# Second layer's decay matrices as one exponential with 0/1 masks in the batches, and later transposes of finished outputs

## The chip, the cores and the metric

One core of a Trainium2 chip. The time is the device time of one launch in microseconds (us), median of three runs. The engines are named as the profile names them: PE (TensorE matmuls), PEld (its weight loads), DVE (VectorE), ACT (ScalarE), POOL (GpSimd), SP (SyncE, which here issues loads).

## What is computed

One step of a two-layer encoder over 1024 prompt frames and 64 sample frames, width 1024, in fp32. The first layer (gated convolution and band attention) is not touched. The second is gated DeltaNet: 8 heads, 17 chunks of 64 frames (16 of the prompt, one of the sample). For a head and chunk, with `gc` the running sum of the log decays:

```
decay = exp(where(l >= m, gc[l] - gc[m], -inf))
a     = where(l > m, beta[l] * (k k^T) * decay, 0)
sol   = solve(I + a, [v * beta, k * beta * exp(gc)])
u     = sol_v - sol_k @ S
qk    = (q k^T) * decay
o     = (q * exp(gc)) @ S + qk @ u
S     = exp(gc[-1]) * S + (k * exp(gc[-1] - gc))^T @ u
y     = rmsnorm(o) * silu(z) @ w_out
```

The gates are negative, so `gc` falls within a chunk, and for l >= m the difference is the negative of its absolute value.

## The kernel before

Everything is transposed: channels on the 128 partitions, the 1088 frames in the free dimension, in three groups of 384, 384 and 320 frames. A projection (`project`, lines around L186) multiplies a 128x1024 weight tile with one group, each fp32 operand split into a high and a low part: per group 24 matmuls, in the profile `pjt<-hhi,whi`, `pjt<-hhi,wlo` and `pjt<-hlo,whi`. These fill TensorE. The weights are split by ScalarE (L164) and VectorE (L165).

The order of TensorE is written by a small planner, `Order`: each piece of work is a generator with a rank and a list of what must be done before it. A piece that yields a number is not looked at again until the plan's own clock (nanoseconds, advanced by an estimate per matmul) has moved on that much; of the pieces that are due, the lowest rank goes next. The projections (`main`, rank 5) fill what the rest leaves. So a number in a `yield` says how many nanoseconds of other TensorE work are planned between two steps. The order of the other engines comes from the framework's scheduler when the program is built; each engine then runs its list in order.

In the second layer (`odd`) the heads go in four pairs (p = 0 to 3), one head on each half of the partitions, and the chunks of a pair in three batches of 6, 6 and 5. The profile calls batch b of pair p number n = 3p + b. Per batch:

- `gates` once at the start makes `gc` and its exponentials (`G`).
- `decays` (L886 on, once for all pairs, rank 3): per pair and batch, VectorE spreads `gc` over an identity (`gx`, L895), TensorE sums it over the rows of a head, which broadcasts it (a matmul into `tr`), VectorE subtracts `gc` (`df`, L899). Then twice: GpSimd adds a mask of 0 and -1e30 (L902), ScalarE takes the exponential (L903), a transfer stores it in HBM (L904, `Dd`). The first result is strictly lower triangular (for `a`), the second is upper triangular with the diagonal (for `qk`, transposed). All of it lives in one buffer, `dbuf`, in parts.
- `prepare` (rank 2; waits for `dec{p}`, the pair's decays): SyncE loads both matrices (`Dst`, `DT`, L930 and L931); TensorE transposes k and q of the batch (`tr<-cst,kq`), ScalarE sums their squares (`junk`, L945) and copies k (`kt`), VectorE makes `kd` (L948), then the reciprocal root of the sums by a shift and three Newton steps of small operations (`rr`, `rt`, L747 to L753), then `sT`, `sA` and `kap`; GpSimd scales `kt` (L957). TensorE multiplies k with k and q (`tr<-kq`, two groups, 8 and 4 or 2 matmuls). VectorE makes `An` from the first half (L966, times `sA` and `Dst`) and `KQD` from the second (L967, times `DT`), and picks the diagonal 16x16 blocks of `An` into `Af` (L971, L973), which go through HBM (`Sd`) to another layout.
- `substitute` inverts those blocks on GpSimd (`px`, `AL`, L991 and L992), `join` builds the 64x64 inverse (`X`, `XT`, `M`), `solve` (`BD`, `vr`) applies it.
- `scan` (rank 1) carries the state S over the chunks (`ks`, `us`, `su`) and makes the outputs `o`, four chunks to a tile `o4` (three buffers); before a fourth tile it waits for the `finish` of the first.
- `finish` (rank 3): VectorE and GpSimd make the reciprocal root for the norm (`so`, L747 to L758), VectorE scales `o` (L1175); then `yield 9000`; then TensorE transposes it (`tr<-cst,o`), ScalarE scales it by the norm's weights (L1183) and it is stored (`od`).

All these share two PSUM buffers named `tr`: TensorE's next write to one waits until the engines that read its last content are done. Dst, DT and (after the change) E have a single buffer in SBUF, `An` two, `KQD` three.

Of the kernel before, what the change touches and what calls it, by code (L numbers as in the profile page):

```python
# [15 lines left out]
P = 128  # L16
# [23 lines left out]
C_M1, C_M2 = 448, 512  # L40
# [16 lines left out]
def constants():  # L57
    c = np.zeros((P, NCONST), np.float32)
    p = np.arange(P)
    h, i = p // 64, p % 64  # L60
    same = h[:, None] == h[None, :]
    c[:, C_ID:C_ID + P] = np.eye(P)
    c[:, C_U:C_U + P] = same & (i[:, None] <= i[None, :])
    c[:, C_BD:C_BD + P] = same
    c[:, C_H:C_H + 2] = h[:, None] == np.arange(2)[None, :]
    j = np.arange(64)
    c[:, C_ID64:C_ID64 + 64] = i[:, None] == j[None, :]
    c[:, C_M1:C_M1 + 64] = np.where(j[None, :] < i[:, None], 0.0, NEG)
    c[:, C_M2:C_M2 + 64] = np.where(j[None, :] >= i[:, None], 0.0, NEG)
    c[:, C_B16:C_B16 + 4] = (i // 16)[:, None] == np.arange(4)[None, :]  # L70
    c[:, C_H16:C_H16 + 2] = (i // 16 % 2)[:, None] == np.arange(2)[None, :]
    return c
# [35 lines left out]
class Net:  # L108
# [121 lines left out]
    def run(self):  # L230
# [4 lines left out]
        with tc.tile_pool(name="pj", bufs=2, space=PSUM) as self.pj:  # L235
# [15 lines left out]
            self.Dd = [dram.tile([P, NCH, 64], F32, name=f"Dd{i}") for i in range(8)]  # L251
# [481 lines left out]
    def odd(self):  # L733
# [147 lines left out]

        def decays():
            gc = G["gc"]
            buf = G["buf"]

            def part(i, m):  # L886
                return buf[:, 384 * i:384 * i + 64 * m].rearrange("p (c j) -> p c j", j=64)

            for p in range(4):
                yield 0  # L890
                for c0, m in BATCHES:
                    sh = [P, m, 64]
                    gcb = gc[:, p, c0:c0 + m].unsqueeze(2).broadcast_to(sh)
                    gx, df = part(0, m), part(1, m)
                    dve.tensor_tensor(gx, gcb, cst[:, C_ID64:C_ID64 + 64].unsqueeze(1).broadcast_to(sh), ALU.mult)  # L895
                    yield 900
                    ps = pst("tr")
                    self.mm(ps[:, :64 * m], cst[:, C_BD:C_BD + P], gx.rearrange("p c j -> p (c j)"))
                    dve.tensor_tensor(df, ps[:, :64 * m].rearrange("p (c j) -> p c j", j=64), gcb, ALU.subtract)  # L899
                    for q, (cm, op) in enumerate(((C_M1, ALU.subtract), (C_M2, ALU.add))):  # L900
                        dx = part(2 + q, m)
                        pool.tensor_tensor(dx, cst[:, cm:cm + 64].unsqueeze(1).broadcast_to(sh), df, op)  # L902
                        act.activation(dx, dx, AF.Exp)  # L903
                        nc.scalar.dma_start(Dd[2 * p + q][:, c0:c0 + m, :], dx)  # L904
# [11 lines left out]
        def prepare(p, b):  # L916
# [3 lines left out]
            yield 4000 if b == 0 else 0  # L920
# [8 lines left out]
            Dst, DT = bt("Dst", 64), bt("DT", 64)  # L929
            nc.sync.dma_start(Dst, Dd[2 * p][:, c0:c0 + nb, :])  # L930
            nc.sync.dma_start(DT, Dd[2 * p + 1][:, c0:c0 + nb, :])  # L931
# [26 lines left out]
            An, KQD = bt("An", 64, 2), bt("KQD", 64, 3)  # L958
            for i0 in range(0, nb, 4):
# [5 lines left out]
                for i in range(m):  # L965
                    dve.scalar_tensor_tensor(An[:, i0 + i, :], ps[:, i, 0:64], sA[:, i0 + i:i0 + i + 1], Dst[:, i0 + i, :], ALU.mult, ALU.mult)  # L966
                dve.tensor_tensor(KQD[:, i0:i0 + m, :], ps[:, :m, 64:128], DT[:, i0:i0 + m, :], ALU.mult)  # L967
# [4 lines left out]
            for j in range(1, 4):  # L972
                dve.scalar_tensor_tensor(Af, An[:, :, 16 * j:16 * j + 16], cst[:, C_B16 + j:C_B16 + j + 1], Af, ALU.mult, ALU.add)  # L973
            sa = Sd[0][b]
# [190 lines left out]
        def finish(p, b, i0, m, o4, so):  # L1165
# [10 lines left out]
            yield 9000  # L1176
# [10 lines left out]
        def add_pair(p):  # L1187
            for b in range(NB):
# [8 lines left out]
                order.add(f"prep{n}", 2, prepare(p, b), [f"dec{p}"] + after("prep", n - 1) + after("wy", n - 2) + after("scan", n - 3))  # L1197
# [136 lines left out]
```

## Time and profile before

| | us |
|---|---|
| median of 3 runs (range) | 1455.97 (1453.89 to 1456.44) |
| profiled execution | 1450.93 |
| its span, first to last instruction | 1449.1 |
| PE busy | 1372.1 |
| DVE busy | 877.6 |
| ACT busy | 678.0 |
| POOL busy | 312.9 |

Times in the profile count from the first instruction of the span. A busy share is an average over stages with different limits, so it is read by stretches. "Idle before" an instruction is put down to the one that released it last. The granted clock is TensorE's, 1.00 being full speed. The second layer's decays run from about 694 us (first `gx`) to 777 us (last store), its last scan ends well before the output projections.

### The profile page before, as it was taken

The numbers are of one execution on the slowest core, as the hardware profiler recorded it, in microseconds if no ns is written. First come the engines' busy times: TensorE is split into PE (matmuls) and PEld (weight loads), VectorE is DVE, ScalarE is ACT, GpSimd is POOL, SyncE is SP. The second block draws the span as 40 slices with busy tenths as digits, with TensorE's granted clock in tenths as the row PEclk, the third lists the DMA queues.
The fourth block names the chain that finished last, engine by engine and source line by source line (L and its number), as shares of the span: only waits on it lengthen the run. The fifth ranks groups of instructions, "written<-read, shape, count | busy, mean of one in ns | idle before, by whom it ended". The sixth has DMA issues, their size and how long they took to land. (4 is left out here: it accounts for less than half of the span.)

```text
span 1449.1 us, 28440 instructions
## 1 busy us (share of the span) xinstructions
PE 1372.1 (95%) x10600; PEld 1233.9 (85%) x10600; DVE 877.6 (61%) x2497; ACT 678.0 (47%) x1776; POOL 312.9 (22%) x810
## 2 busy tenths in 40 slices
PE   8999999999999999899878999999899989998996
PEld 6989998998999899888768778788887877888985
DVE  7675257137435754777887768676765756433654
ACT  7643345144334456675546444544453534323642
POOL 3000000000100014420345325140523152210322
PEclk9999999999999999999989999999999999999998
DMA  7402111210210274541523112122211232337454
GB/s 260 143 16 89 57 52 52 80 53 26 90 61 30 66 244 135 190 140 37 119 73 79 40 29 77 33 52 44 68 30 31 62 95 67 95 123 234 141 197 162
DMA packets 114378, 133.12 MB, mean 92 GB/s; under 512 B 35568, under 2 KB 81336, under 8 KB 114240
## 3 DMA queue, kind: packets, MB, share of 16 engines
q1 hardware_dynamic: 83280, 105.01, 24.8%
q10 hardware_dynamic: 30960, 26.31, 5.6%
q8 instruction: 83, 1.36, 0.4%
q14 instruction: 55, 0.45, 0.1%
HBM read 99.91 MB, written 34.51 MB: 93 GB/s over the span
## 5 line engine op out<-in xcount | busy, mean ns | idle before, releaser
L119 PE MATMUL pjt<-hhi,wlo 128*128 128x384 f32 (+1 forms) x1768 | 617.7, 349 | 1.5 <-DVE wlo L165 1.5
L119 PE MATMUL pjt<-hhi,whi 128*128 128x384 f32 (+1 forms) x1768 | 583.7, 330 | 5.8 <-ACT whi L164 2.4
L119 PE MATMUL pjt<-hlo,whi 128*128 128x384 f32 (+1 forms) x1768 | 576.1, 330 | 0.7 <-DVE hlo L391 0.6
L119 PEld LDWEIGHTS pjt<-hhi,wlo 128*128 128x128 f32 x1768 | 337.6, 191 | 25.6 <-issue 11.7
L119 PEld LDWEIGHTS pjt<-hhi,whi 128*128 128x128 f32 x1768 | 337.6, 191 | 12.4 <-ACT whi L164 3.7
L119 PEld LDWEIGHTS pjt<-hlo,whi 128*128 128x128 f32 x1768 | 335.6, 190 | 1.8 <-DVE hlo L391 1.8
L165 DVE TENSOR_TENSOR wlo<-wf,whi 128x512 fp32r<-128x512 f32 x222 | 154.3, 721 | 153.0 <-ACT whi L164 149.5
L164 ACT CAST whi<-wf 128x512 fp32r<-128x512 f32 x222 | 129.6, 618 | 165.0 <-PE pjt L119 123.4
L612 ACT ACTIVATE pr<-pr,mx 128x640 f32<-128x640 f32 (+5 forms) x72 | 50.9, 707 | 89.4 <-DVE mx L611 88.9
L784 DVE SCALAR_TENSOR_TENSOR kq<-pjt,par,kq 128x384 f32<-128x384 f32 (+2 forms) x144 | 71.6, 497 | 2.9
L348 POOL TENSOR_TENSOR sqa<-sqa,sq 128x384 f32<-128x384 f32 (+1 forms) x36 | 39.7, 1103 | 151.7 <-ACT sq L346 151.6
L573 POOL MEMSET bias<- 64x64 f32 x8 | 1.3, 163 | 321.0 <-DMA bias<-Gd 228.2
L609 DVE CUSTOM_DVE_ANT_0 pr<-sc,bias 128x640 f32<-128x640 f32 (+5 forms) x72 | 48.0, 666 | 26.7 <-PE sc L119 25.9
L991 POOL TENSOR_TENSOR px<-AL 48x14 f32<-48x14 f32 (+6 forms) x168 | 46.9, 279 | 61.5 <-DMA AL<-Sd 52.5
L1154 DVE SCALAR_TENSOR_TENSOR S<-S,egl,su 128x128 f32<-128x128 f32 x128 | 40.6, 343 | 29.3 <-PE su L119 28.9
L755 POOL TENSOR_TENSOR so<-so 128x4 f32<-128x4 f32 (+2 forms) x72 | 16.7, 232 | 175.4 <-DVE so L748 117.2
L945 ACT ACTIVATE junk<-tr 128x128 f32<-128x128 f32 x136 | 37.7, 277 | 33.9 <-PE tr L124 29.6
L992 POOL TENSOR_TENSOR AL<-AL,px 48x14 f32<-48x14 f32 (+6 forms) x168 | 46.8, 278 | 9.4
L119 PE MATMUL pjt<-mhi,whi 128*128 128x384 f32 x128 | 44.4, 347 | 3.7 <-ACT mhi L164 3.7
L124 PE MATMUL pt<-cst,pr 128*128 128x128 f32 (+1 forms) x280 | 43.4, 270 | 4.5 <-DVE pr L614 2.9
L1113 ACT ACTIVATE junk<-o 128x128 f32<-128x128 f32 x68 | 21.0, 309 | 51.4 <-DVE o L1109 42.2
L119 PE MATMUL pjt<-mlo,whi 128*128 128x384 f32 x128 | 44.5, 348 | 0.3 <-DVE mlo L165 0.2
(250 smaller groups left out, 2210.8 us busy)
## 6 DMA issues: line engine op xcount, KB each, us to landing
wf<-in_w_in SPq DMA_DIRECT2D x128, 256.0 KB, 3.5
wf<-in_w_out SPq DMA_DIRECT2D x96, 256.0 KB, 3.5
mf<-mixd SPq DMA_DIRECT2D x32, 192.0 KB, 3.4
x<-in_x SPq DMA_DIRECT2D x8, 384.0 KB, 6.2
xg<-in_x SPq DMA_DIRECT2D x2, 1536.0 KB
xd<-xg SPq DMA_DIRECT2D x2, 1536.0 KB
Dd<-dbuf ACTq DMA_DIRECT2D x16, 192.0 KB, 2.1
od<-o ACTq DMA_DIRECT2D x12, 256.0 KB, 2.5
```

The costliest lines, as they stand in the source:

```text
L119: return self.pe.matmul(out, lhsT=lhsT, rhs=rhs, start=start, stop=stop, **k)
L124: return self.pe.transpose(out, in_, self.ident[0:k, 0:k])
L164: self.act.copy(out=hi, in_=x)
L165: (eng or self.dve).tensor_tensor(lo, x, hi.bitcast(F32), ALU.subtract)
L348: pool.tensor_tensor(acc, acc, sq, ALU.add)
L609: dve.tensor_tensor_reduce(out=cut(pr[0:nq, :nk]), in0=sc[0:nq, :nk // nw, :nw], in1=cut(b["bias"][a][0:nq, j0:j0 + nk]), scale=1.0, scala ...
L612: act.activation(pr[0:nq, :nk], pr[0:nq, :nk], AF.Exp, bias=mx[0:nq, 1:2], scale=1.0, accum_out=mx[0:nq, 2:3])
L784: dve.scalar_tensor_tensor(oi, ch(ps[:, i0 + j + 1:i0 + j + 1 + m]), cw[j], oi, ALU.mult, ALU.add)
L945: act.activation(junk, ps[:, i, :], AF.Square, accum_out=ss[:, a, i0 + i:i0 + i + 1])
L991: pool.tensor_tensor(t, AL[:, j + 1:16, j:j + 1].broadcast_to([lanes, m, w]), x.broadcast_to([lanes, m, w]), ALU.mult)
L992: pool.tensor_tensor(o, o, t, ALU.add)
L1154: dve.scalar_tensor_tensor(Sn[:, q, :], S[:, q, :], egl[:, q, p, c:c + 1], su[q], ALU.mult, ALU.add)
```

## The change

Since the decay is symmetric up to the mask, `decay` now makes one matrix E = exp(-|difference|) per pair and batch: the same spread, matmul and subtraction, but the difference stays in PSUM (written in place), ScalarE takes its absolute value and then the exponential; no mask. For the pairs 1 to 3 it is made in `decays` and goes through HBM as before, one store (L905) and one load (L932) instead of two. For the pair 0 `prepare` makes it itself, with `An` as scratch for `gx`, and so waits for `gates` only.

The masks are now 0 and 1 and are multiplied: GpSimd makes `KQD` = E times the upper mask (L963) ahead of VectorE's product with q k^T; `An` takes E unmasked, and the strict lower mask is applied to `Af`, whose 16x16 blocks are the only place where it matters (the other blocks that are used lie wholly below the diagonal). And `finish` waits 15000 instead of 9000 before its transposes, but for the last batch.

```diff
-    c[:, C_M1:C_M1 + 64] = np.where(j[None, :] < i[:, None], 0.0, NEG)
-    c[:, C_M2:C_M2 + 64] = np.where(j[None, :] >= i[:, None], 0.0, NEG)
+    c[:, C_LOW:C_LOW + 16] = j[None, :16] < (i % 16)[:, None]
+    c[:, C_UP:C_UP + 64] = j[None, :] >= i[:, None]
...
+        def decay(e, gx, p, c0, m):
+            sh = [P, m, 64]
+            gcb = G["gc"][:, p, c0:c0 + m].unsqueeze(2).broadcast_to(sh)
+            dve.tensor_tensor(gx, gcb, cst[:, C_ID64:C_ID64 + 64].unsqueeze(1).broadcast_to(sh), ALU.mult)
+            yield 900
+            ps = pst("tr")[:, :64 * m]
+            self.mm(ps, cst[:, C_BD:C_BD + P], gx.rearrange("p c j -> p (c j)"))
+            ps = ps.rearrange("p (c j) -> p c j", j=64)
+            dve.tensor_tensor(ps, ps, gcb, ALU.subtract)
+            act.activation(e, ps, AF.Abs)
+            act.activation(e, e, AF.Exp, scale=-1.0)
...
-            for p in range(4):
-                yield 0
+            for p in range(1, 4):
                 for c0, m in BATCHES:
...
-                    dve.tensor_tensor(df, ps[:, :64 * m].rearrange("p (c j) -> p c j", j=64), gcb, ALU.subtract)
-                    for q, (cm, op) in enumerate(((C_M1, ALU.subtract), (C_M2, ALU.add))):
-                        dx = part(2 + q, m)
-                        pool.tensor_tensor(dx, cst[:, cm:cm + 64].unsqueeze(1).broadcast_to(sh), df, op)
-                        act.activation(dx, dx, AF.Exp)
-                        nc.scalar.dma_start(Dd[2 * p + q][:, c0:c0 + m, :], dx)
+                    e = piece(2 + i % 3, m)
+                    yield from decay(e, piece(i % 2, m), p, c0, m)
+                    nc.scalar.dma_start(Dd[p][:, c0:c0 + m, :], e)
+                    i += 1
                     yield 2500
...
-            yield 4000 if b == 0 else 0
...
-            Dst, DT = bt("Dst", 64), bt("DT", 64)
-            nc.sync.dma_start(Dst, Dd[2 * p][:, c0:c0 + nb, :])
-            nc.sync.dma_start(DT, Dd[2 * p + 1][:, c0:c0 + nb, :])
+            E, An, KQD = bt("E", 64), bt("An", 64, 2), bt("KQD", 64, 3)
+            if p:
+                nc.sync.dma_start(E, Dd[p][:, c0:c0 + nb, :])
+            else:
+                yield from decay(E, An, p, c0, nb)
+            if b == 0:
+                yield 4000
...
-            An, KQD = bt("An", 64, 2), bt("KQD", 64, 3)
+            pool.tensor_tensor(KQD, E, cst[:, C_UP:C_UP + 64].unsqueeze(1).broadcast_to([P, nb, 64]), ALU.mult)
...
-                dve.tensor_tensor(KQD[:, i0:i0 + m, :], ps[:, :m, 64:128], DT[:, i0:i0 + m, :], ALU.mult)
+                dve.tensor_tensor(KQD[:, i0:i0 + m, :], ps[:, :m, 64:128], KQD[:, i0:i0 + m, :], ALU.mult)
...
+            dve.tensor_tensor(Af, Af, cst[:, C_LOW:C_LOW + 16].unsqueeze(1).broadcast_to([P, nb, 16]), ALU.mult)
...
-            yield 9000
+            yield 9000 if p == 3 and b == NB - 1 else 15000
...
-                order.add(f"prep{n}", 2, prepare(p, b), [f"dec{p}"] + after("prep", n - 1) + after("wy", n - 2) + after("scan", n - 3))
+                order.add(f"prep{n}", 2, prepare(p, b), [f"dec{p}" if p else "gates"] + after("prep", n - 1) + after("wy", n - 2) + after("scan", n - 3))
```

More of the change, by code (lines that the diff above doesn't have):

```diff
@@ L39 @@
 C_ID64 = 384
-C_M1, C_M2 = 448, 512
+C_LOW, C_UP = 448, 512
 C_B16 = 576
@@ L250, in run @@
             self.Gd = [dram.tile([P, LROW], F32, name=f"Gd{h}") for h in range(8)]
-            self.Dd = [dram.tile([P, NCH, 64], F32, name=f"Dd{i}") for i in range(8)]
+            self.Dd = [dram.tile([P, NCH, 64], F32, name=f"Dd{i}") for i in range(4)]
             self.Sd = [[dram.tile([m, P, 16], F32, name=f"Sd{a}{b}") for b, (c0, m) in enumerate(BATCHES)] for a in range(2)]
@@ L880, in gates, with piece @@
             yield 1500
+        def decay(e, gx, p, c0, m):
[9 more added lines that the diff above has]
+            act.activation(e, e, AF.Exp, scale=-1.0)
         def decays():
-            gc = G["gc"]
-            buf = G["buf"]
-            def part(i, m):
+            buf, i = G["buf"], 0
+            def piece(i, m):
                 return buf[:, 384 * i:384 * i + 64 * m].rearrange("p (c j) -> p c j", j=64)
-            for p in range(4):
-                yield 0
+            for p in range(1, 4):
                 for c0, m in BATCHES:
[L892 to L899, printed above, removed]
-                    for q, (cm, op) in enumerate(((C_M1, ALU.subtract), (C_M2, ALU.add))):
-                        dx = part(2 + q, m)
-                        pool.tensor_tensor(dx, cst[:, cm:cm + 64].unsqueeze(1).broadcast_to(sh), df, op)
-                        act.activation(dx, dx, AF.Exp)
-                        nc.scalar.dma_start(Dd[2 * p + q][:, c0:c0 + m, :], dx)
+                    e = piece(2 + i % 3, m)
+                    yield from decay(e, piece(i % 2, m), p, c0, m)
+                    nc.scalar.dma_start(Dd[p][:, c0:c0 + m, :], e)
+                    i += 1
                     yield 2500
@@ L965, in prepare @@
                 for i in range(m):
-                    dve.scalar_tensor_tensor(An[:, i0 + i, :], ps[:, i, 0:64], sA[:, i0 + i:i0 + i + 1], Dst[:, i0 + i, :], ALU.mult, ALU.mult)
-                dve.tensor_tensor(KQD[:, i0:i0 + m, :], ps[:, :m, 64:128], DT[:, i0:i0 + m, :], ALU.mult)
+                    dve.scalar_tensor_tensor(An[:, i0 + i, :], ps[:, i, 0:64], sA[:, i0 + i:i0 + i + 1], E[:, i0 + i, :], ALU.mult, ALU.mult)
+                dve.tensor_tensor(KQD[:, i0:i0 + m, :], ps[:, :m, 64:128], KQD[:, i0:i0 + m, :], ALU.mult)
                 yield 510
```

## The prediction

> **What bounds the kernel now.** First the page's busy shares, then the chain that ended last, then a table by stretches of the second layer, then TensorE's waits in each stretch.
>
> ```profile
> PE 1372.1 (95%) x10600; PEld 1233.9 (85%) x10600; DVE 877.6 (61%) x2497; ACT 678.0 (47%) x1776; POOL 312.9 (22%) x810
> PE 9%; DMA 3%; DVE 2%; ACT 1%; issue 0%; DVEq 0%; SPq 0%; ACTq 0%
> ```
>
> TensorE is busy for 95% of the span and its order is fixed when the program is built. The chain is only the tail. So the end moves by what TensorE loses: stalls in its order, and time at a reduced clock. The change leaves TensorE's work alone (the same matmuls and transposes), so I look where it loses. In the windows below the columns are length, then busy time and count of each engine, then the granted clock. The first stretch, 689 to 777 us, is where the old decays run (their first and last masked operands fall in it); the second is the rest of the batches.
>
> ```profile
> 689.00:777.00 88.00, 71.35 (x398) 63.53 (x397) 71.56 (x180) 44.91 (x124) 37.78 (x61) 0.90 0.40 97
> 777.00:1240.00 463.00, 441.69 (x4558) 368.33 (x4559) 311.41 (x1146) 213.66 (x727) 152.90 (x586) 0.99 0.23 54
> 721.70:725.10 3.40, 3.40 (x12) 3.34 (x11) 3.19 (x10) 1.93 (x8) 1.26 (x1) 0.50 0.52 181
> 738.80:742.20 3.40, 2.95 (x10) 2.38 (x10) 2.22 (x9) 1.77 (x10) 0.00 (x0) 0.50 0.36 116
> 749.00:752.40 3.40, 3.40 (x13) 3.40 (x12) 2.69 (x9) 1.82 (x7) 0.94 (x1) 0.50 0.76 75
> 762.70:769.50 6.80, 4.75 (x14) 4.17 (x15) 5.86 (x20) 3.43 (x6) 5.89 (x13) 0.50 0.25 77
> 1172.72:1175.70 2.98, 2.98 (x11) 2.94 (x12) 0.82 (x5) 0.84 (x2) 0.21 (x1) 0.50 0.73 136
> ```
>
> The first stretch loses 88.00 - 71.35 = 16.65 us to stalls in 88 us; the second loses 21.3 us in 463. Four windows of the first stretch, 17.0 us together, ran at clock 0.50; TensorE was busy in 14.5 us of them (3.40 + 2.95 + 3.40 + 4.75), so they cost half of that, 7.25 us. The last row is one such window in the second stretch: 2.98 us at half speed, 1.5 us lost. Who is waited for, in the first stretch and then in the second:
>
> ```profile
> PE tr L119 <- DVE KQD L967: 4.5, 1, 4.5
> PE tr L124 <- DVE dbuf L899: 4.0, 2, 2.6
> PE tr L124 <- DVE KQD L967: 3.4, 1, 3.4
> PE tr L119 <- DVE dbuf L895: 2.6, 2, 1.6
> PE tr L119 <- ACT junk L945: 1.5, 2, 0.9
> ...
> PE tr L124 <- DVE o L1175: 4.4, 2, 3.1
> PE su L119 <- DVE us L1140: 3.3, 2, 2.6
> PE tr L119 <- POOL AL L992: 2.6, 1, 2.6
> ```
>
> Nearly all are waits for one of the two PSUM buffers named `tr`, held until VectorE has read it. VectorE is late in that stretch (busy 71.56 of 88). Why, the groups of VectorE and GpSimd show, for the first stretch and then (the rows after the dots) for the second:
>
> ```profile
> L899 DVE TENSOR_TENSOR dbuf<-tr,gc 128x384 f32<-128x384 f32 x8 | 4.4, 555 | 3.2 <-PE tr L119 2.4 <-POOL dbuf L902 0.8
> L752 DVE TENSOR_TENSOR rt<-rt,rr 128x12 f32<-128x12 f32 x6 | 4.3, 710 | 0.1
> L753 DVE SCALAR_TENSOR_TENSOR rr<-rt,rr 128x12 f32<-128x12 f32 x6 | 2.0, 327 | 0.2
> L902 POOL TENSOR_TENSOR dbuf<-cst,dbuf 128x384 f32<-128x384 f32 x16 | 18.2, 1153 | 62.5 <-DVE dbuf L899 54.4 <-DMA Dd<-dbuf 7.7 <-issue 0.3
> L902 POOL TENSOR_TENSOR dbuf<-cst,dbuf 128x320 f32<-128x320 f32 x8 | 8.0, 1016 | 13.9 <-DVE dbuf L899 8.8 <-ACT whi L164 3.4 <-DMA Dd<-dbuf 1.7
> L903 ACT ACTIVATE dbuf<-dbuf 128x384 f32<-128x384 f32 x16 | 8.4, 525 | 15.1 <-POOL dbuf L902 15.0
> ...
> L752 DVE TENSOR_TENSOR rt<-rt,rr 128x12 f32<-128x12 f32 x18 | 3.3, 183 | 0.2
> L753 DVE SCALAR_TENSOR_TENSOR rr<-rt,rr 128x12 f32<-128x12 f32 x18 | 3.2, 177 | 0.3
> ```
>
> A twelve-column product takes 183 ns where there are no decays and 710 ns beside them. One case in the timeline (start, length) shows how:
>
> ```profile
> 759.41 2.47 DVE L752 TENSOR_TENSOR rt<-rt,rr 128x12 f32<-128x12 f32 x1
> ...
> 759.65 0.99 POOL L902 TENSOR_TENSOR dbuf<-cst,dbuf 128x384 f32<-128x384 f32 x1
> 760.61 0.28 POOL L991 TENSOR_TENSOR px<-AL 48x56 f32<-48x56 f32 x1
> 760.86 0.99 POOL L902 TENSOR_TENSOR dbuf<-cst,dbuf 128x384 f32<-128x384 f32 x1
> ...
> 764.75 1.62 PE L119 MATMUL tr<-dbuf,cst 128*128 128x384 f32 x2 [4.54 <-DVE KQD L967]
> ```
>
> The product ends when GpSimd's run of masked decays ends; behind it stand the rest of the root, `sA`, `An` and `KQD`, and TensorE waits 4.54 us for that `KQD`. L899, which reads PSUM, shows no such stretching (555 ns).
>
> **The change, part by part.** *GpSimd's masked decays* go: 24 operations, 18.2 + 8.0 = 26.2 us of GpSimd, 12 of the 24 exponentials and 15 of the 24 stores. What TensorE sees of it is VectorE's delay in the two roots before the waited-for `KQD`: 6 x (710 - 183) = 3.2 us and 6 x (327 - 177) = 0.9 us, 4.1 us of the 4.5 + 3.4 = 7.9.
>
> Part of this is handed back by the order. TensorE, first batch, between the last products k·k, q·k (`tr<-kq`, four of them) and the next batch's transposes (`tr<-cst,kq`), before:
>
> ```order
> L119 MATMUL tr<-kq 64x128 x4
> L119 MATMUL pjt<-hhi_6899,wlo 128x320
> L119 MATMUL pjt<-hhi_6899,whi 128x320
> L119 MATMUL pjt<-hlo_6900,whi 128x320
> L119 MATMUL pjt<-hhi_6899,wlo 128x320
> L119 MATMUL pjt<-hhi_6899,whi 128x320
> L119 MATMUL pjt<-hlo_6900,whi 128x320
> L124 MATMUL tr<-cst,kq 128x128 x4
> ```
>
> And after, with the decay matmuls of the third pair (`dbuf`) and of the first pair's second batch (`An`, used as scratch):
>
> ```order
> L119 MATMUL tr<-kq 64x128 x4
> L119 MATMUL tr<-dbuf,cst 128x320
> L119 MATMUL pjt<-hhi_6045,wlo 128x384
> L119 MATMUL pjt<-hhi_6045,whi 128x384
> L119 MATMUL pjt<-hlo_6046,whi 128x384
> L119 MATMUL pjt<-hhi_6045,wlo 128x384
> L119 MATMUL pjt<-hhi_6045,whi 128x384
> L119 MATMUL pjt<-hlo_6046,whi 128x384
> L119 MATMUL tr<-An,cst 128x384
> L124 MATMUL tr<-cst,kq 128x128 x4
> ```
>
> The `dbuf` matmul now asks for the buffer that `KQD` still holds six projection matmuls sooner, and the transposes ask for the one that the decay has just filled. Projection matmuls start 0.17 us apart:
>
> ```profile
> 780.22 0.33 PE L119 MATMUL pjt<-hhi,whi 128*128 128x384 f32 x1
> 780.39 0.33 PE L119 MATMUL pjt<-hlo,whi 128*128 128x384 f32 x1
> ```
>
> So six are 1.0 us; for the second batch I take 0.9. Left of the `KQD` waits: 7.9 - 4.1 + 1.9 = 5.7 us (bounds 2 and 7.9).
>
> *The subtraction in place.* The 4.0 us for L899 came of VectorE waiting for GpSimd to release the difference (0.8 of idle in its row) and standing late. Now it is written into PSUM, GpSimd does not read it, and the buffer is held until ScalarE's absolute value is done: 0.555 + about 0.525 us (L903 as the nearest row for a 384-column activation) plus ScalarE's queue, busy 44.91 of 88. Left: 2.0 us (bounds 0 and 6, twelve decays at half a microsecond more each). Of L895's 2.6 us the first 1.0 stays, since nothing ahead of it changes; the junk wait and small rest, 16.65 - 7.9 - 4.0 - 2.6 = 2.15 us, stay. Left in all: 5.7 + 2.0 + 1.0 + 2.2 = 10.9, saved **5.8 us**.
>
> *The clock.* The four half-speed windows stand at the stalls of 2.6, 3.4, 1.4 (4.0 - 2.6) and 4.5 us. I take the loss in proportion to the stalls left, 10.9 / 16.65 = 0.65: 4.7 of 7.25 us stays, saved **2.5 us** (bounds 0 and 7.25). The Trainium skill (TensorE: Matmul & The Clock Gate, HAM oscillation) says that the clock falls after an idle gap above about 3.4 us. By that rule the windows at the shorter stalls would not have been slow; the trace differs, since the one at 721.70 stands behind this stall:
>
> ```profile
> 720.47 0.66 PE L124 MATMUL tr<-cst,kq 128*128 128x128 f32 x4 [2.57 <-DVE dbuf L899]
> ```
>
> *First pair's decays in the batches.* Three batches lose the wait for their decays and the load of them. They gain the six instructions of `decay` each, on engines with idle time; of all pairs together, 15 store issues leave ScalarE's queue and 15 loads SyncE's, where they stood among the weight loads. TensorE's total is the same; this alone I cost at nothing, since the projections fill the place (if the cover failed: one decay matmul and its chain, 1 to 2 us).
>
> *The later transposes.* TensorE reaches them 6 us later on the plan's clock (15000 for 9000), and the two waits behind them are shorter than that:
>
> ```profile
> 1172.72 1.11 PE L124 MATMUL tr<-cst,o 128*128 128x128 f32 x4 [3.08 <-DVE o L1175]
> 1179.70 0.30 PE L124 MATMUL tr<-cst,o 128*128 128x128 f32 x1 [1.30 <-DVE o L1175]
> ```
>
> Both go, 4.4 us, and with the first the half-speed window at 1172.72, 1.5 us: saved **5.9 us** (bounds 0 and 5.9). Next late there may be the scan, which waits for a free `o4` buffer (three); the last batch keeps 9000, so the tail does not grow.
>
> *Masks as products.* Twelve products on GpSimd, priced by L902 at 1.15 us, ten of them in the second stretch; twelve small ones on VectorE ahead of the solve (0.26 us by the first row below), which TensorE does not wait for directly. The nearest row for what a wide GpSimd product does to VectorE in the second stretch is `kt`: the operation that runs beside it goes from 258 to 489 ns on the mean:
>
> ```profile
> L971 DVE TENSOR_SCALAR Af<-An,cst 128x96 f32<-128x96 f32 x2 | 0.5, 258 | 0.0
> ...
> L971 DVE TENSOR_SCALAR Af<-An,cst 128x96 f32<-128x96 f32 x6 | 2.9, 489 | 0.0
> ```
>
> That is 1.4 us over six; I charge **1.5 us** (bounds 0 and 10 x 1.15 = 11.5). The Trainium skill (SBUF — State Buffer, Who interferes with whom) speaks against this part: a VectorE operation with two SBUF inputs and a reading GpSimd operation exclude one another. The trace agrees so far as L752 (both operands in SBUF) is stretched and L899 (one in PSUM) is not. By the rule alone each of the ten masks could hold VectorE for its whole length, an estimate of 11.5 us in place of 1.5.
>
> Sum: -5.8 - 2.5 - 5.9 + 1.5 = **-12.7 us**. The profiled execution took 1450.93 us (span 1449.1), 5.0 below the median of the runs shown, so 1438.2 on its scale and 1455.97 - 12.7 = **1443.3** on that of the median.
>
> **The rivals.**
>
> 1. *The stage keeps its stalls* because the buffer waits for ScalarE: twelve holds of 0.5 us or more replace what left, and the clock with them. For it: the last order rows, transposes right behind a decay. Against: ScalarE loses as many exponentials as it gains absolute values. Then only the transposes pay: -5.9 + 1.5 = -4.4, 1451.6.
> 2. *Nothing measurable*: TensorE meets the next late operand of the same chain wherever one stall goes: 1456. Against: the first stretch loses 19% to stalls and the second 5%, with the same steps per batch in both.
> 3. *Slower: GpSimd's queue.* Its place, in the last pair, behind the second batch's `kt`, among the roots of finished outputs (`so`) and the solve (`px`, `AL`). GpSimd before:
>
> ```order
> L758 TENSOR_TENSOR so<-so 128x4
> L992 TENSOR_TENSOR AL<-AL,px 48x2x13
> L755 TENSOR_TENSOR so<-so 128x4
> L957 TENSOR_TENSOR kt<-kt,kap 128x768
> L991 TENSOR_TENSOR px<-AL 48x14
> L756 TENSOR_TENSOR so<-so 128x4
> ```
>
> And after, a few rows behind that `kt`:
>
> ```order
> L755 TENSOR_TENSOR so<-so 128x4
> L755 TENSOR_TENSOR so<-so 128x1
> L998 TENSOR_TENSOR AL<-AL,px 48x5x10
> L756 TENSOR_TENSOR so<-so 128x4
> L756 TENSOR_TENSOR so<-so 128x1
> L997 TENSOR_TENSOR px<-AL 48x44
> L963 TENSOR_TENSOR KQD<-E,cst 128x320
> L757 TENSOR_SCALAR so<-so 128x4
> ```
>
> The third batch's mask now stands in the middle of that work. It waits for a load into the single buffer `E`, free only when the batch ahead has used it; the old load of the same size landed this much after its issue (minimum, median, maximum):
>
> ```profile
> DMA to landing us min/median/max: 2.2/2.5/2.8
> ```
>
> The rest of the solve and the roots queue behind. One such wait on TensorE was 2.6 us (`AL` above), with a slow window 4.1. Four of them in the ten later batches outweigh the gain (16.4 against 12.7); six give 1455.97 + 24.6 - 12.7 = 1467.9. Against: the roots have 6 us more now, and the solve rarely was what TensorE waited for (once in 463 us).
> 4. *No slow window left.* If the clock falls only after stalls longer than any that is left, the other 4.7 us is saved too: 1438.6. The stall of 2.57 us with its window at 721.70 speaks against. (This is what the rule of the Trainium skill, TensorE: Matmul & The Clock Gate, cited above, would give.)
>
> **How the numbers follow.** Forecast 0.60; rival 1 0.14; rival 2 0.08; rival 3 0.12; rival 4 0.06. A measurement of this kernel can tell about 0.2%, 2.9 us, from no change. Faster: 0.60 + 0.14 + 0.06 = 0.80; same 0.08; slower 0.12. The range: low, the terms at their good bounds (stalls 5.9 + 4.0 + 1.6 = 11.5, clock 7.25, transposes 5.9), 1455.97 - 24.65 = 1431; high 1453, past rival 1. Rivals 2 and 3, 0.20, lie outside.
>
> **What would show it.** Right: in the stretch of the decays TensorE idle near 11 us instead of 16.65, L752 near 0.18 us there, clock above 0.92; no wait of the transposes of `o` on VectorE near the end of the third pair. Wrong: waits of TensorE on the absolute value or on `AL` in GpSimd's column, GpSimd idle before the mask for a DMA, or a second stretch that loses more than 21 us.

## The result, and the profile after

The changed kernel is slower by half a per cent: 1462.05 us median of 20 runs (1458.2 to 1465.75) beside 1454.04 us for the kernel before (20 runs), a ratio of 1.0055, 95% interval [1.004, 1.007]. I had forecast 1443.3 (range 1431 to 1453). The profiled execution took 1460.29 us, its span 1458.5.

First the shares of the page and the chain of the changed kernel, in which little has changed (GpSimd is busy for 18.9 us less, VectorE for 7.5 us less):

```profile
PE 1372.8 (94%) x10600; PEld 1234.0 (85%) x10600; DVE 870.1 (60%) x2509; ACT 677.7 (46%) x1774; POOL 294.0 (20%) x798
PE 10%; DMA 3%; DVE 2%; ACT 1%; issue 0%; DVEq 0%; SPq 0%; ACTq 0%
```

So the question is again what TensorE loses. The same two stretches as in the prediction, then windows at five of its stalls (length, busy time and count of PE, PEld, DVE, ACT, POOL, granted clock, DMA share, GB/s):

```profile
689.00:777.00 88.00, 78.10 (x601) 70.37 (x600) 66.49 (x203) 44.93 (x131) 22.88 (x66) 0.94 0.23 61
777.00:1240.00 463.00, 433.42 (x4350) 361.16 (x4349) 307.61 (x1134) 210.81 (x712) 148.53 (x569) 0.98 0.20 48
726.40:729.80 3.40, 3.40 (x10) 2.79 (x11) 2.80 (x12) 0.91 (x2) 0.03 (x1) 0.60 0.00 0
759.00:765.80 6.80, 6.80 (x93) 6.26 (x93) 4.46 (x13) 1.92 (x5) 2.77 (x11) 0.58 0.09 15
892.80:896.20 3.40, 3.40 (x13) 3.37 (x14) 1.44 (x8) 1.20 (x3) 1.37 (x8) 0.50 0.21 70
1034.31:1037.73 3.42, 2.76 (x10) 2.76 (x11) 1.50 (x8) 1.29 (x3) 1.49 (x7) 0.50 0.25 46
1176.00:1180.50 4.50, 4.50 (x16) 4.46 (x17) 1.44 (x8) 1.44 (x4) 1.37 (x8) 0.50 0.28 76
```

The stretch of the decays idles for 88.00 - 78.10 = 9.9 us, near the forecast (10.9; before 16.65), at clock 0.94 (before 0.90). The second stretch idles for 29.6 us instead of 21.3, at clock 0.98 instead of 0.99. The waits in the first stretch and, behind the dots, the largest of the whole span, then the four cases of that largest one in TensorE's timeline:

```profile
PE tr L119 <- DVE KQD L972: 3.4, 1, 3.4
PE tr L119 <- issue: 2.6, 1, 2.6
PE tr L119 <- ACT dbuf L892: 1.3, 1, 1.3
PE tr L119 <- DVE dbuf L886: 1.1, 1, 1.1
PE tr L124 <- ACT dbuf L892: 0.9, 1, 0.9
...
PE tr L124 <- DVE o L1181: 18.9, 4, 6.8
```

```profile
892.74 1.09 PE L124 MATMUL tr<-cst,o 128*128 128x128 f32 x4 [5.86 <-DVE o L1181]
1034.97 1.09 PE L124 MATMUL tr<-cst,o 128*128 128x128 f32 x4 [4.24 <-DVE o L1181]
1175.94 1.09 PE L124 MATMUL tr<-cst,o 128*128 128x128 f32 x4 [6.77 <-DVE o L1181]
1301.96 0.30 PE L124 MATMUL tr<-cst,o 128*128 128x128 f32 x1 [2.00 <-DVE o L1181]
```

The transposes of finished outputs, which I expected to wait no more, wait 18.9 us where they waited 4.4. The first three cases are the same place three times: the first tile (four chunks) of the third batch of the first, second and third pair. At each stands a window at half speed.

What makes that output late is seen at the first place, in VectorE's timeline (start, length), which makes the tile's fourth output, and in ScalarE's, which squares it:

```profile
869.32 0.29 DVE L1115 TENSOR_TENSOR o<-tr,qs 128x128 f32<-128x128 f32 x1
```

```profile
877.79 0.28 ACT L950 ACTIVATE junk<-tr 128x128 f32<-128x128 f32 x1 [1.45 <-PE tr L124]
878.47 0.27 ACT L950 ACTIVATE junk<-tr 128x128 f32<-128x128 f32 x1
878.86 0.31 ACT L1119 ACTIVATE junk<-o 128x128 f32<-128x128 f32 x1
879.63 0.30 ACT L1119 ACTIVATE junk<-o 128x128 f32<-128x128 f32 x1
```

The output was ready at 869.61, but its square (L1119 at 878.86) stands in ScalarE's list behind the keys' squares of the next batch (L950), with which it shares the one-buffer tile `junk`; so it comes 9 us late, and the square of the fifth output follows 0.8 us behind it (879.63). Two roots (`so`) then run on GpSimd together. GpSimd's timeline at that place, before and after:

```profile
867.41 1.47 POOL L957 TENSOR_TENSOR kt<-kt,kap 128x768 f32<-128x768 f32 x1 [12.64 <-DVE sA L955]
875.97 0.21 POOL L991 TENSOR_TENSOR px<-AL 48x14 f32<-48x14 f32 x1 [7.09 <-DMA AL<-Sd]
...
885.17 0.21 POOL L992 TENSOR_TENSOR AL<-AL,px 48x14 f32<-48x14 f32 x1
885.35 1.47 POOL L957 TENSOR_TENSOR kt<-kt,kap 128x768 f32<-128x768 f32 x1
```

```profile
865.92 1.47 POOL L962 TENSOR_TENSOR kt<-kt,kap 128x768 f32<-128x768 f32 x1 [26.27 <-DVE sA L960]
879.33 0.21 POOL L997 TENSOR_TENSOR px<-AL 48x14 f32<-48x14 f32 x1 [7.45 <-DMA AL<-Sd]
882.88 0.19 POOL L755 TENSOR_TENSOR so<-so 128x4 f32<-128x4 f32 x1
886.92 1.46 POOL L962 TENSOR_TENSOR kt<-kt,kap 128x768 f32<-128x768 f32 x1
890.52 0.85 POOL L963 TENSOR_TENSOR KQD<-E,cst 128x320 f32<-128x320 f32 x1
891.87 0.34 POOL L758 TENSOR_TENSOR so<-so 128x4 f32<-128x4 f32 x2
894.04 0.21 POOL L998 TENSOR_TENSOR AL<-AL,px 48x14 f32<-48x14 f32 x1
```

Before, GpSimd has the 28 rows of the second pair's first substitute (`px`, `AL`) to itself, 875.97 to 885.4, and the next `kt` follows. After, the rows start 13.4 us behind `kt` instead of 8.6 and run among two roots, the next `kt` and a mask, 879.33 to 894.3. Both the output (root finished at 892.2) and the substitute (`XT`, which it leads to) come late there.

Over the whole of the batches, from 669 us to the last transposes of outputs, before and after:

```profile
669.00:1298.00 629.00, 590.53 (x5629) 499.40 (x5627) 423.20 (x1452) 285.26 (x923) 202.57 (x696) 0.98 0.26 63
```

```profile
669.00:1302.00 633.00, 590.00 (x5630) 499.54 (x5629) 417.13 (x1472) 287.51 (x928) 183.09 (x684) 0.98 0.22 54
```

Idle 38.5 before, 43.0 after. The rest of the 9.4 us between the spans is in the tail (156.5 against 151.1 us). In a second profiled execution of the changed kernel (after_again, below) it is the other way: the stretch took 638 us (46.4 idle) and the tail 151.8. So 4 to 9 us of the loss lie in the batches, and what the tail adds is not steady.

### The profile page after: what moved, and what is told of

It is laid out like the page before. It is cut to its first block, busy times and chain, and to the rows that moved or that the text cites. A ratio compares the mean times of both kernels' runs of the same rounds, so it can differ in the third digit from the quotient of the medians.

```text
span 1458.5 us, 28364 instructions
## 1 busy us (share of the span) xinstructions
PE 1372.8 (94%) x10600; PEld 1234.0 (85%) x10600; DVE 870.1 (60%) x2509; ACT 677.7 (46%) x1774; POOL 294.0 (20%) x798
## 5 line engine op out<-in xcount | busy, mean ns | idle before, releaser
L950 ACT ACTIVATE junk<-tr 128x128 f32<-128x128 f32 x136 | 37.7, 277 | 33.1 <-PE tr L124 30.1
L1119 ACT ACTIVATE junk<-o 128x128 f32<-128x128 f32 x68 | 21.0, 309 | 61.3 <-DVE o L1115 43.3
```

Of the source, the lines that this page charges most:

```text
L950: act.activation(junk, ps[:, i, :], AF.Square, accum_out=ss[:, a, i0 + i:i0 + i + 1])
```

## The experiments

Each ratio is against the kernel before on the same chip, from 5 to 12 runs of the one (20 of the change) and 11 to 30 of the other. "Stretch" runs from 669 us to the last transposes of outputs; idle is its length less TensorE's busy time; "on o" and "on XT" are TensorE's waits for finished outputs and for the substitute's result. Some expectations count more as a wait on outputs, all idle time ahead of a transpose of outputs (12.7 for late_only, 26.5 for decays_only). The last three columns come from one execution each; the change's own two executions differ by 5 us of stretch and 3.4 us of idle, so smaller differences between rows say nothing.

| kernel | ratio [95%] | stretch, idle us | on o | on XT |
|---|---|---|---|---|
| before | 1 | 629, 38.5 | 4.4 | - |
| the change | 1.0055 [1.004, 1.007] | 633, 43.0 | 18.9 | 0.6 |
| after_again | 1.0031 [1.0013, 1.0048] | 638, 46.4 | 18.0 | 1.0 |
| late_only | 1.0027 [1.0008, 1.0045] | 637, 50.0 | 9.7 | 4.5 |
| decays_only | 1.0119 [1.0092, 1.0146] | 652, 56.2 | 24.2 | - |
| root_dve | 1.0038 [1.0018, 1.0058] | 640, 45.2 | 7.7 | 10.8 |
| mask_dve | 1.0016 [0.9998, 1.0034] | 642, 47.7 | 18.1 | 0.9 |
| junk_after | 1.0114 [1.0089, 1.0139] | 651, 52.2 | 2.0 | 21.2 |
| junk_decays | 1.0032 [1.0013, 1.0051] | 642, 48.2 | 8.9 | 9.1 |
| junk_before16 | 1.0008 [0.9989, 1.0026] | 640, 43.4 | 5.5 | 1.0 |
| junk_late16 | 1.0044 [1.0025, 1.0063] | 645, 48.7 | 2.7 | 7.5 |
| after_early | 1.0062 [1.0029, 1.0094] | 648, 48.6 | 17.3 | - |
| fold | 0.9997 [0.9979, 1.0014] | 636, 41.4 | 19.1 | 0.6 |
| fold_early | 1.0015 [0.999, 1.0039] | 635, 39.9 | 15.9 | - |
| e2 | 1.0014 [0.9995, 1.0032] | 644, 47.5 | 17.9 | - |
| p0_dram | 0.9993 [0.9972, 1.0015] | 630, 39.1 | 8.4 | 2.5 |
| junk_fold_early | 1.0061 [1.0038, 1.0085] | 639, 43.0 | 2.3 | 10.8 |
| p0_nolate | 0.9924 [0.9899, 0.9948] | 624, 37.0 | 9.6 | - |
| p0_jfe | 1.0071 [1.0051, 1.0091] | 642, 53.0 | 2.0 | 6.7 |
| margin | 1.0071 [1.0044, 1.0099] | 645, 50.8 | 12.4 | - |

**The two halves alone.** late_only is the kernel before with this edit, decays_only the changed kernel with its reverse:

```
-            yield 9000
+            yield 9000 if p == 3 and b == NB - 1 else 15000
```

> The kernel before with nothing but the later transposes of the finished outputs (15000 in place of 9000). If the two halves hurt each other (the shifted batches bring two roots and a mask together on GpSimd, and the transposes then wait for their outputs), GpSimd's order here is nearly that of before: the 4.4 us that the transposes waited for outputs go to under 1, nothing else moves by more than 1 or 2, 1448 to 1453. If the later transposes lose time by themselves, for instance because work that filled a gap has left it, 1458 or more. If they do nothing, 1454.

> The changed kernel with the transposes of the finished outputs where they stood before (9000): one exponential, the masks, the first pair's decays in its batches. If the masks and the shifted batches load GpSimd, the roots are late here too, and with 6 us less of distance each of the three third batches waits longer: over 30 us of waits of the transposes on outputs, 1465 to 1475. If the two halves hurt only together, the stage's gain of 7 us of stalls stays and the waits on outputs are those of before: 1445 to 1449. If the decays half loses time elsewhere, 1458 to 1462 with few waits on outputs.

Measured 1.0027 and 1.0119. Neither half is a gain by itself; the later transposes lose 0.3% where I had them at -5.9 us, the decays half loses 1.2%, and together they lose less than the second alone. By TensorE's waits in the two (9.7 and 24.2 us on outputs in the table) the later transposes do shorten the waits on outputs that the decays half makes (24.2 to 18.9), and lengthen them in the kernel before (4.4 to 9.7). The loss begins in the decays half.

**Work taken off GpSimd.** root_dve has the roots of outputs on VectorE, mask_dve the second mask:

```
-            rsqrt(fa, va, tm, pool)
+            rsqrt(fa, va, tm, dve)
```
```
-            pool.tensor_tensor(KQD, E, cst[:, C_UP:C_UP + 64]...
+            dve.tensor_tensor(KQD, E, cst[:, C_UP:C_UP + 64]...
```

> The changed kernel with the root of each finished output on VectorE instead of GpSimd (nine small operations of some 0.2 us in place of twelve of 0.35 us, nothing else moved). If two roots that share GpSimd's queue with the substitute's rows and the masks make the three long waits, the 18.9 us on outputs fall under 6 and the time to 1447 to 1453. If the squares on ScalarE come too late by themselves, the waits fall by less than 8 us and the time stays above 1455. If VectorE in turn holds what TensorE needs, waits on other tiles of VectorE grow by what those on outputs lose, and the time stays near 1462.

> The changed kernel with the mask of the second decays as a product on VectorE instead of GpSimd. If the mask that stands among the roots is what makes the outputs late, the three long waits lose most of their 17 us: 1448 to 1455. If it is the two roots and the substitute's rows, each wait loses at most the mask's 0.85 us: some 2.5 us in all, and VectorE gets twelve products more: 1458 to 1463.

Measured 1.0038 and 1.0016. The mask is not it: the waits on outputs stay at 18.1. Without the roots on GpSimd they fall to 7.7, and TensorE waits for `XT` instead:

```profile
PE tr L119 <- DVE XT L1027: 10.8, 3, 7.8
PE tr L124 <- DVE o L1181: 7.7, 4, 2.8
```

The longest of these, 7.8 us, is my third rival at work, once: the third batch's mask stands in the middle of the rows and waits for its load.

```profile
1042.07 0.86 POOL L963 TENSOR_TENSOR KQD<-E,cst 128x320 f32<-128x320 f32 x1 [6.14 <-DMA E<-Dd]
```

**A tile of their own for the outputs' squares** (theory A: the shared `junk` makes them late). There is room for it in the changed kernel; in the kernel before both tiles had to be bfloat16 to fit.

```
-                junk = self.kp.tile([P, P], F32, name="junk", tag="junk", bufs=1)
-                act.activation(junk, o4[:, a, :], AF.Square, accum_out=so[:, 0, a:a + 1])
+                sq = self.kp.tile([P, P], F32, name="sq", tag="sq", bufs=1)
+                act.activation(sq, o4[:, a, :], AF.Square, accum_out=so[:, 0, a:a + 1])
```

> The changed kernel in which the squares of the outputs write their unused elements to a tile of their own (sq) instead of the one tile, junk, that they share with the squares of the keys and queries; TensorE's order is word for word the same. Theory A: in the third batches the squares of the fourth and the fifth output both wait until the keys' squares have given junk back, so that both roots run together and late; with sq the fourth square runs right behind its output, some 5 to 9 us sooner, the two roots run apart, the waits of the transposes on outputs fall from 18.9 to under 6 us and nothing takes their place: 0.993 to 0.998 of the kernel before. Theory B: GpSimd's queue is full with the substitute's rows, kt, the masks and the loads of E, and whoever is late there passes the wait on, as with the root on VectorE: the waits on outputs fall, but those on XT or KQD grow by as much, 1.002 to 1.006.

> The same tile of their own for the outputs' squares, with the transposes of the outputs where they stood before (9000). Theory A: most of the 26.5 us of waits on outputs go, but with 6 us less of distance 5 to 8 stay: 0.996 to 1.002 of the kernel before (1.012 without the tile). Theory B: 1.008 or more.

> The kernel before with a tile of their own for the outputs' squares; there is no room for two tiles of float32, so both unused tiles are bfloat16 (the sums stay float32). Here the fourth and fifth squares ran 5 us apart and the waits on outputs are 6.5 us. Theory A: they fall to 2 to 4, 0.996 to 0.999 of the kernel before. Theory B: 1.000.

> The kernel before with both bfloat16 tiles and the later transposes (15000). Theory A: the waits on outputs, 12.7 us with the later transposes alone, go to under 4, and the time from 1.003 to 0.995 to 0.999 of the kernel before. Theory B: 1.002 to 1.004, as without the tiles.

Theory A fell, though its mechanism is there. In junk_after the fourth square runs at 875.11 instead of 878.86, 0.8 us behind its output instead of 9 (the output itself comes 4.7 us later), the waits on outputs go from 18.9 to 2.0, as it says, and the kernel is slower by a further half per cent. TensorE's timeline at the first of the three places:

```profile
904.46 0.84 PE L119 MATMUL tr<-XT,Cb 32*32 32x16 f32 x48 [8.15 <-DVE XT L1027]
```

The wait has moved one step down TensorE's list, from the outputs to `XT`, and grown. Only junk_decays gained (1.0119 to 1.0032); junk_before16 gave 1.0008 beside 1, junk_late16 1.0044 beside late_only's 1.0027.

**The chain to the substitute** (theory C). after_early writes the rows of `Af` directly behind the last `An`; fold takes the mask of `Af` away and puts it into the constant by which `X` is multiplied; fold_early does both; e2 gives `E` two buffers.

```
-                yield 510
+                if i0 + m < nb:
+                    yield 510
```
```
-            dve.tensor_tensor(Af, Af, cst[:, C_LOW:C_LOW + 16]..., ALU.mult)
...
-                m = cst[:, C_H16 + j:C_H16 + j + 1].unsqueeze(2)...
+                m = cst[:, C_LOW + 16 * j:C_LOW + 16 * j + 16].unsqueeze(1)...
```
```
-            E, An, KQD = bt("E", 64), ...
+            E, An, KQD = bt("E", 64, 2), ...
```

> The changed kernel in which the rows that fold An into Af are written directly behind the last An of a batch and not 510 behind it: on VectorE they then stand ahead of wlo, kd and three vt of the convolution; nothing else is changed. Theory C: TensorE waits at the third batches because the next pair's first batch comes late through its chain (An, Af, the write and read of AL, the substitute's rows on GpSimd, X, XT): from kt to XT 34 us in the changed kernel, 23 to 30 before, most of the first part lost on VectorE between An and Af (8.1 to 8.6 us from kt to the write of Af; 4.3 to 5.4 before). Here the write of Af comes 3 to 4 us sooner, the rows are through before the next kt, the roots and the mask come between them, and the long waits (18.9 us on outputs) fall under 7: 0.993 to 0.999 of the kernel before. Theory B (GpSimd's queue holds too much at that place, whoever comes first): waits pass to XT or to the outputs as before, 1.002 to 1.012.

> The changed kernel without the product that masks Af: the mask stands in the constant with which X is multiplied in any case (the substitute reads only what lies below the diagonal). One row of 0.25 us less on VectorE in the chain to XT, with some 0.6 us of waiting for its turn. Theory C: the write of Af comes 0.9 us sooner in each batch, which is not enough to bring the rows ahead of the roots: the waits fall by 1 to 5 us, 1.001 to 1.005. If this added row is by itself what broke the order, 0.994 to 0.998. Theory B: 1.005.

> Both: the mask in the constant of X and the rows of Af directly behind An. Theory C: 0.992 to 0.998, at most 2 us below the kernel with the rows moved alone. Theory B: 1.002 to 1.012.

> The changed kernel with two buffers for E, so that the load of the next batch's decays waits for no An and the weights' loads and the write of Af stand behind no waiting load on SyncE, and the mask doesn't hold GpSimd for its data (15 us of GpSimd's waits). Theory C: GpSimd's waits for E were idle time that nobody waited for; kt to XT stays 32 to 34 us, 1.003 to 1.007. My third rival (the mask's load holds the substitute's rows): the rows start 3 us sooner, the long waits fall by half or more, 0.995 to 1.000.

Theory C fell too: after_early sends `Af` off 6.1 us behind `kt` at the first place instead of 8.1, and the waits on outputs stay at 17.3 (1.0062). e2 takes GpSimd's waits for `E` away (15.1 us in the change) and leaves those on outputs at 17.9, so GpSimd's waits for `E` are not what makes the outputs late. fold is the best of this group (0.9997), with the waits on outputs unchanged (19.1); what it gained, beside after_again's 1.0031 on another chip, is 0.3%, about the sum of the two intervals' half widths, and not more. The same holds for fold_early (1.0015, waits on outputs 15.9), e2 (1.0014) and mask_dve above (1.0016): none of them is shown to be faster than the change.

**Both chains at once, and the first pair's decays back in DRAM.** junk_fold_early has the own tile, the folded mask and the early `Af` together. p0_dram undoes one part of the change:

```
-            for p in range(1, 4):
+            for p in range(4):
...
-            if p:
-                nc.sync.dma_start(E, Dd[p][:, c0:c0 + nb, :])
-            else:
-                yield from decay(E, An, p, c0, nb)
+            nc.sync.dma_start(E, Dd[p][:, c0:c0 + nb, :])
...
-    [f"dec{p}" if p else "gates"]
+    [f"dec{p}"]
```

> The changed kernel as it is, on the chip and beside the runs of the kernel before that the next two are measured with. Every theory: 1.004 to 1.007 of the kernel before, as in the result; if it is nearer to 1.002, the gains of the versions with the folded mask, with two buffers for E and with the mask on VectorE (0.9997 to 1.0016, measured beside other runs) are smaller than they seem.

> The changed kernel with the first pair's decays taken back out of its batches: all four pairs' decays are made ahead, kept in DRAM and read back; one exponential, masks and the later transposes stay. Theory F: the first pair's decays in the batches bring all later batches ahead against the projections, and so the squares of the third batches' fourth outputs behind the next keys' squares; without that GpSimd does the substitute's rows of the second pair ahead of the roots, the waits on outputs fall under 10 us, and the stage loses 3 to 6 us of its gain: 0.998 to 1.002. Theory C (the added row and the order on VectorE between An and Af are enough, wherever the batches stand): the waits stay over 15 us, 1.004 to 1.010.

> The changed kernel with three edits together: the outputs' squares in a tile of their own, the mask of Af in the constant of X, and the rows of Af directly behind An. Each alone passed the wait on: squares sooner, and TensorE waited for XT (21 us); Af sooner, and it waited for the outputs (16 to 19 us). Theory G (two chains come late at the same place of TensorE's list, and the later of the two sets the wait): together the waits on outputs and on XT fall under 8 us in sum: 0.992 to 0.997 of the kernel before. Theory B (GpSimd's queue holds too much work there in any order): 12 us or more of waits on the two, 1.000 to 1.010.

The control gave 1.0031. p0_dram gave 0.9993 beside it: the first pair's decays in the batches cost about 0.4% (1461.2 against 1454.89 us, both beside 1456.06). Of the three long waits on outputs the third pair's stays (5.7 us; the other 2.7 us are the last batch's), the first pair's and the second pair's are gone, and at the second pair's place TensorE waits 2.5 us for `XT`, much as theory F has it; p0_dram and then junk_fold_early:

```profile
PE tr L124 <- DVE o L1178: 8.4, 2, 5.7
```

```profile
PE tr L120 <- DVE XT L1028: 10.8, 2, 6.1
...
PE tr L125 <- DVE o L1182: 2.3, 1, 2.3
```

junk_fold_early (1.0061) ends theory G: the waits on outputs fall to 2.3, those on `XT` rise to 10.8. Theory B gave this ratio, but it is not shown either: with the roots off GpSimd (root_dve) nothing was gained.

**What is left: three versions.** p0_nolate is p0_dram with the transposes at 9000: one exponential and masks alone. p0_jfe is p0_dram with the three edits of junk_fold_early. margin gives the three places longer distances in TensorE's list:

```
-            yield 6500
+            yield 12500 if p and b == 0 else 6500
...
+            ... else 21000 if b == NB - 1 and i0 == 0 else 15000
```

> The changed kernel with the first pair's decays back in DRAM and the transposes of the outputs where they stood before: one exponential and the masks alone. Theory F (the two halves meet only where the first pair's decays in the batches have moved the batches): with the batches near their old places GpSimd has the rows of the second and third pair's first batch to itself, the waits on outputs are 4 to 10 us as before: 0.995 to 1.000 of the kernel before; decays_only, which has the first pair's decays in its batches besides, gave 1.012. Theory C (the added row on VectorE and the masks are enough): 1.004 or more.

> The changed kernel with the first pair's decays back in DRAM, and with the three edits to the chain (own tile for the squares, mask of Af in X's constant, Af directly behind An). GpSimd's list has two of the three critical substitutes free of roots and kt. Theory F with G: waits on outputs and XT under 8 us, 0.993 to 0.998. Theory B: waits pass on to whatever comes next, 0.999 to 1.006.

> The changed kernel with longer distances in TensorE's list at the three places alone: 6000 more ahead of the transposes of the first tile of each third batch, and 6000 more between the write of Af and the work on the substitute of the next pair's first batch. Theory H (the list's distances are fixed and shorter than the chains take there, 34 us from kt to XT; other work of TensorE is at hand to fill 6 us): the waits on outputs and XT at the three places fall from 19 to under 6 us: 0.992 to 0.999. If the batches' own chain (scan, next keys, substitute, solve, scan) sets the time there, the 6 us come back as waits elsewhere or as a later end of the scans: 1.002 to 1.010.

p0_nolate is faster than both kernels: 1448.4 us median of 6 runs beside 1460.92 for the kernel before (11 runs), 0.9924 [0.9899, 0.9948]. Its batches, and its one long wait on an output:

```profile
669.00:1293.00 624.00, 587.03 (x5618) 497.23 (x5617) 413.93 (x1460) 285.24 (x922) 189.07 (x684) 0.98 0.24 56
```

```profile
1168.72 1.11 PE L124 MATMUL tr<-cst,o 128*128 128x128 f32 x4 [8.54 <-DVE o L1178]
```

margin (1.0071) ends theory H. At the three places the longer distances did what was asked of them, 6.1 us of waits on outputs for 16.9, and yet the stretch became 7 to 12 us longer than the change's (645 against 638 and 633): waits on the last pair's outputs (6.4 us), on `vt` (6.0) and on the state (2.7) came in. p0_jfe (1.0071) shows the same of the three edits of junk_fold_early: against p0_dram the waits on outputs fall from 8.4 to 2.0, those on `XT` rise from 2.5 to 6.7, and the stretch idles for 53.0 us instead of 39.1.

With three of the parts as factors, the ratios are:

| | transposes at 9000 | at 15000 |
|---|---|---|
| decays as before | 1 | 1.0027 |
| one exponential, masks, all pairs through DRAM | 0.9924 | 0.9993 |
| the same, first pair in its batches (the change) | 1.0119 | 1.0055 and 1.0031 |

The one exponential with masks gains 0.8%. The first pair's decays in the batches lose 2.0% at 9000 and about 0.4% at 15000. The later transposes lose 0.3% and 0.7% in the first two rows and gain 0.6% to 0.9% in the third, where there is a loss to win back. Where these figures compare ratios from different chips, they are larger than the 0.24% by which the change itself came out differently on two chips.

What the two parts do to TensorE's list can be counted in the traces: the projection matmuls that stand ahead of a batch's first product of k with k. In p0_nolate all twelve counts are those of before (3393, 3456 and 3615 in the first pair). The first pair's decays in its batches move every one: in the changed kernel they are 36, 33 and 51 fewer in the first pair, 9, 30 and 21 more in the second, 15, 24 and 39 fewer in the third, and 6, 9 and 9 more in the last. So theory F's "ahead" holds for two pairs only; the others come later. With the batches where they were, GpSimd has most of the second pair's first substitute to itself again: in p0_nolate its rows run from 866.59 to 877.4 with only a `kt` among them, and the first root starts at 883.09. The fourth and the fifth square are 5.6 us apart instead of 0.8, and TensorE waits 1.1 us for the outputs there instead of 5.9.

## Why the prediction was wrong, point by point

- *The stage of the decays*: right. Stalls 9.9 us for 10.9 (12.0 in after_again). The `KQD` waits 3.4 (I left 5.7), the buffers held by VectorE's subtraction and then by ScalarE's absolute value 1.3 + 0.9 (2.0), L886 1.1 (1.0). The small rest that I left at 2.2 was 0.6 us, but for a wait that I had not seen, `issue` 2.6. That VectorE's small products were stretched by GpSimd's masked decays is borne out; the same group in the same stretch, 710 ns before, and behind the dots three groups of the second stretch:

```profile
L752 DVE TENSOR_TENSOR rt<-rt,rr 128x12 f32<-128x12 f32 x6 | 1.0, 167 | 0.0
...
L752 DVE TENSOR_TENSOR rt<-rt,rr 128x12 f32<-128x12 f32 x18 | 3.0, 168 | 0.4
L979 DVE TENSOR_TENSOR Af<-Af,cst 128x80 f32<-128x80 f32 x4 | 2.2, 560 | 0.0
L979 DVE TENSOR_TENSOR Af<-Af,cst 128x96 f32<-128x96 f32 x6 | 1.5, 249 | 0.0
```

- *The clock there*: right, 0.94 (0.96 in after_again) for the "above 0.92".
- *The masks as products, +1.5 us*: not too small. p0_nolate carries all twelve and gains 0.8% (11 us on 1455.97; my terms for it, -5.8 - 2.5 + 1.5, make 6.8). In the second stretch L752 runs at its usual length (168 ns). The mean of 560 ns for the four added products of 80 columns hides two of 0.23 us and two of 0.89 and 0.88 us that stand beside a mask; here is one:

```profile
942.72 1.03 POOL L963 TENSOR_TENSOR KQD<-E,cst 128x384 f32<-128x384 f32 x1 [3.26 <-PE tr L119]
942.96 0.89 DVE L979 TENSOR_TENSOR Af<-Af,cst 128x80 f32<-128x80 f32 x1
```

With a product of L978 at 1032.20 (1.05 us for a usual 0.31) they lose 2.1 us; at the other seven masks of that stretch no VectorE operation is held by more than 0.1 us. The Trainium skill (SBUF — State Buffer, Who interferes with whom) says that a VectorE operation with two SBUF inputs and a reading GpSimd operation exclude one another; the trace agrees, since the three are of this kind and end 0.1 us behind their mask. The estimate of 11.5 us that I drew from it is not borne out, because at only three of the ten masks was there such an operation to hold.
- *The later transposes, -5.9 us*: this step failed, and in sign. I took two waits of 3.08 and 1.30 us from the trace of before and let 6 us of distance cover them. Alone in the kernel before the edit costs 0.3%; on top of one exponential and masks 0.7%. The waits on outputs were not a fixed lateness against which distance could be set. In late_only the first of the two grew from 3.1 to 7.0 us and `XT` came in with 4.5 us. The list moves with the distance: the third pair's batches stand 9, 12 and 30 projection matmuls earlier than before.
- *First pair's decays in the batches, at nothing*: this step failed as well, and it turned the sign. "The projections fill the place" holds for the decays themselves (the first stretch idles for 9.9 us in the change and in p0_dram, 10.1 in p0_nolate); what I did not price is that every batch then stands at another point of TensorE's list, by up to 51 projection matmuls, and so meets the scans, the squares and GpSimd's rows elsewhere. That costs 0.4% with the transposes at 15000 and 2.0% at 9000.
- *The rivals*: the third, with 0.12, had the outcome (slower), the place (the second substitute behind the next `kt`, with roots and a mask among its rows) and 1467.9 us for a measured 1462.05. Its mechanism was not what decided: TensorE waited for outputs and not for `AL`, and with two buffers for `E` it waited as long. I had marked the sight that would prove me wrong, a second stretch that loses more than 21 us (what it lost before, 21.3): it lost 29.6. The second, with 0.08, had more of the mechanism: TensorE met the next late operand wherever a stall went, but at a loss and not at no change. The first fell with the stage's stalls (9.9 us for 16.65), the fourth with the half-speed window that a stall of 2.6 us still had there (759.00 in the table above).

What is shown: the one exponential with masks gains, and the loss comes from the other two parts. The first pair's decays in the batches cost the most (2.0% alone), and they move every batch in TensorE's list; the later transposes cost 0.7% alone and take part of the loss back beside them. What is argued from the traces alone: that the moved list costs time by bringing a substitute, two roots, `kt` and a mask together on GpSimd. No edit at a single one of these took the waits away; most moved them. What stays open: why the third pair's third batch waits 5.7 to 8.5 us in the versions with the first pair's decays in DRAM too, and how much of the tail's difference between two executions belongs to the change.

## What to carry to other kernels

Where one engine works through a list fixed at build time, price a change of order by the list and not by the wait that it means to remove: take each part alone and in pairs, since here -0.8% and +2.0% stood behind one diff. A wait that only changes its name when its releaser is made faster (outputs, then `XT`, then `KQD`) says that several chains are late together; then undo what brought them together, rather than speed up one of them. Moving work out of a stage into "free" places is not free when every later step moves with it.

## What the runs showed of the hardware

A half-speed window does not need a long stall. In p0_nolate this one followed a stall of 2.08 us:

```profile
1103.07 1.08 PE L119 MATMUL ks<-S,kq 128*64 128x128 f32 x8 [2.08 <-DVE so L748]
```

```profile
1103.90:1107.30 3.40, 3.40 (x13) 2.57 (x12) 1.10 (x4) 1.07 (x4) 1.78 (x9) 0.54 0.00 0
```

That is another 1.6 us (3.40 us at 0.54). But a window does not come with every stall of this length. The same wait for `KQD`, at the same place of the same program, in the two executions of the changed kernel (first the change, then after_again with the window around it):

```profile
1011.43 0.63 PE L124 MATMUL tr<-cst,kq 128*128 128x128 f32 x4 [2.69 <-DVE KQD L972]
1013.31 0.66 PE L124 MATMUL tr<-cst,kq 128*128 128x128 f32 x2 [2.68 <-DVE KQD L972]
1012.42:1019.25 6.83, 5.94 (x27) 4.43 (x27) 5.38 (x20) 2.32 (x10) 0.56 (x1) 0.50 0.45 107
```

In the first TensorE was granted its full clock (1.00 from 1008.70 to 1034.00), in the second it lost some 3.0 us (half of the 5.94 us in which it was busy). So a stall that is moved and not removed can take a window along, and one execution does not tell whether it will.
